# PSUM banks of three mixers in two pairs, a new plan for their steps, and one norm for both halves of the linear attention

## The chip, the cores and the metric

The kernel runs on one core of a Trainium2 chip. The metric is the device time of one launch in microseconds (us), 803.68 as the median of three runs before the change (801.09, 803.68 and 803.68). A core has the engines TensorE (PE, matmuls; PEld is its weight load), VectorE (DVE), ScalarE (ACT), GpSimd (POOL) and SyncE (SP, which here only starts transfers). Each engine works through its own list of instructions in order. Matmuls write PSUM, which here is eight banks of 128 partitions x 512 numbers; everything else lies in SBUF.

## The reference, cut to what matters

Two layers run over 256 tokens of width 1024. In each, one normed input is projected to 3 groups of columns; three mixers work on them, and their outputs, 512 wide each, are joined and projected back. A gated feed-forward and a gated side input follow.

```python
for i in range(2):
    a = rms_norm(h, attn_norm[i])
    (da_q, da_k, da_v, ssd_z, ssd_xbc, ssd_dt, gla_q, gla_k, gla_v, gla_g, gla_lr) = split(a @ w_in[i])
    y_da  = diff_attention(...)  # 4 heads: softmax(q1 k1) - lam * softmax(q2 k2), causal, times v, rms_norm
    y_ssd = ssd_mixer(...)       # state-space scan, 2 chunks of 128 tokens
    y_gla = gla_mixer(...)       # linear attention with decay, 4 heads of 128, 4 chunks of 64 tokens
    h = h + concat(y_da, y_ssd, y_gla) @ w_out[i]
    f = rms_norm(h, ffn_norm[i])
    h = h + (silu(f @ w_ffn_gate[i]) * (f @ w_ffn_up[i])) @ w_ffn_down[i]
    h = h + sigmoid(h @ ple_w_gate[i]) * (p[i] @ ple_w_proj[i])

# the end of gla_mixer; o is (tokens, 4 heads, 128)
o = rms_norm(o, g_norm) * silu(g_out)      # the mean square is over the 128 numbers of a head
```

## The kernel before

All weights come from memory as fp32 and are split on the core: ScalarE copies a tile to a rounded high part `wh` (L214), VectorE subtracts to get the low part `wl` (L215). Both have six buffers, so a split waits until the matmuls of an older tile have read theirs. A projection unit is a run of matmuls with high and low parts into one of four PSUM banks tagged `acc` (lines L242 to L265 and L884 to L886, by unit). The units follow each other without a pause when nothing holds them, and the mixers' work is laid between them.

The mixers are Python generators: `da` (the differential attention), `ssd` (the state-space scan) and `gla` (the linear attention, with a step of its own for the decays, L740 to L756). Each `yield` ends a step. The table `PLAN` names the units of the input projection in order and, for each, which mixer goes on one step after which of the unit's pieces (`-` is none); `PLAN_OUT` does so for the units of the output projection. So the tables set the order in which the work is issued; a scheduler then makes each engine's list from it, with small moves for what is marked `soon()`, and gives out buffers. An instruction that needs a buffer waits until the last reader of that buffer is done.

The mixers' matmuls write four PSUM banks tagged `mix` (`bank()`, names `pm`), used in turn by all three. The steps that matter here, with their names:

- `ssd` transposes its inputs (L599, one bank), which VectorE reads at L601 and L602. Later it multiplies (L639) and VectorE finishes at L644 and L645.
- the decays: a triangular matmul (L752) into one bank, which ScalarE reads twice, with a table load for the exponential before the first (`ex` L755, `ei` L756).
- `gla`: scores (L772) into two banks `pa`; chunk states (L790) into three banks `pst`, which VectorE reads one after the other (L804 for the first, L802 for the others, L807 scales); the output in two banks `po` (L817 within the chunk, L826 from the states); norm and gate; transposes (L845); then high and low part of the four `mix` tiles (L409 on ScalarE, L410 on VectorE), which the output projection reads at L256.
- `da`: score units u1 (rows 0 to 127, four heads), u2 and u3 (rows 128 to 255, two heads each). Each writes two banks `pb`, one per softmax, with 64-row matmuls L484 that go to the two banks in turn, and a mask (L491); VectorE takes the maxima (L499), ScalarE the exponentials `e` (L504), VectorE scales and subtracts (L507 to L512). The result is transposed (L469), copied to `at` (L471) and multiplied with `v` (L536, L540, L541) into the bank `y`; norm; transposes (L526); mix parts.

The norm of a bank is `head_norm`: a square on ScalarE (L395), a sum over each head (L397), then 1/sqrt on VectorE by twelve small operations on 128x4 numbers (L184 to L194), and one multiplication of 128x512 numbers (L402). `gla` calls it for each of its two banks and multiplies by the gate afterwards (L837, two halves each).

```python
for e in range(2):
    yn = head_norm(po[e])
    for b in range(2):
        y = yn.rearrange("p (j b d) -> p j b d", j=2, b=2)[:, :, b]
        g = sg[b].rearrange("p (j e d) -> p j e d", j=2, e=2)[:, :, e]
        dve.tensor_tensor(y, y, g, ALU.mult)
    ys.append(yn)
```

Of the kernel before, what the change touches and what calls it, by code (L numbers as in the profile page):

```python
# [10 lines left out]
F32 = mybir.dt.float32  # L11
# [9 lines left out]
P = 128  # L21
# [64 lines left out]
    ('gv0', ('ssd',)),  # L86
    ('gv1', ('gla', '-', '-', 'da', 'da')),
    ('sg0', ('gla', 'ssd', 'gla')),
    ('sg1', ('-', 'da', 'ssd')),
    ('v0', ('ssd', '-', 'da', '-', 'da')),  # L90
    ('v1', ('ssd', 'da', '-', 'gla')),
    ('ple', ('da', '-', '-', 'da', '-', 'gla')),
]
PLAN_OUT = [('-', '-', 'da'), ('-', '-', 'da'), ('-', '-', 'da'), (), (), ()]


def _two_pi_parts():
# [11 lines left out]
def trunk_kernel(ctx: ExitStack, tc: tile.TileContext, a: dict):  # L109
# [21 lines left out]
    def bank_acc():  # L131
        return ps.tile([P, 512], F32, tag="acc", bufs=NACC, name=nm("acc"))

    def bank():
        return ps.tile([P, 512], F32, tag="mix", bufs=8 - NACC, name=nm("pm"))

    def v3(ap, n):
        return ap.rearrange("p (a b) -> p a b", a=n)
# [278 lines left out]
    def da_gen(i, S):  # L417
# [55 lines left out]

        for qb, heads in units:
            nh, nk = len(heads), P * (qb + 1)
            pb = [bank(), bank()]
            for j, hd in enumerate(heads):
                q, k = qk[hd // 2], qk[2 + hd // 2]
                o = (hd % 2) * T

                for n, (a_, b_) in enumerate(((0, 0), (0, 1), (1, 0))):
                    for c in range(2):
                        r = slice(64 * c, 64 * c + 64)
                        pe.matmul(pb[c][:, j * nk:(j + 1) * nk], q[a_][r, o + qb * P:o + (qb + 1) * P],  # L484
                                  k[b_][r, o:o + nk], start=j == 0 and n == 0, stop=False,
                                  skip_group_check=True)
                if j < nh - 1:
                    yield 'part'
            for c in range(2):

                pe.matmul(v3(pb[c], nh)[:, :, nk - P:], idb, negb.unsqueeze(1).to_broadcast([P, nh, P]),  # L491
                          start=False, stop=True, skip_group_check=True)
            if len(es_of) == 2:
                yield 'part'
                attn_t(es_of[0])
            mx = small("mx", [P, 2, 4])
            es, sm = [], small("sm", [P, 2, 4])
            for c in range(2):
                dve.tensor_reduce(mx[:, c, :nh], v3(pb[c], nh), AX.X, ALU.max)  # L499
            dve.tensor_scalar(mx[:, :, :nh], mx[:, :, :nh], -0.125, None, op0=ALU.mult)  # L500
            for c in range(2):
                e = slot("e")
                for j in range(nh):
                    act.activation(e[:, j * nk:(j + 1) * nk], pb[c][:, j * nk:(j + 1) * nk], AF.Exp,  # L504
                                   bias=mx[:, c, j:j + 1], scale=0.125, accum_out=sm[:, c, j:j + 1])
                es.append(e)
            dve.reciprocal(sm[:, :, :nh], sm[:, :, :nh])  # L507
            dve.tensor_scalar(sm[:, 1, :nh], sm[:, 1, :nh], lam[:, i:i + 1], None, op0=ALU.mult)
            for j in range(nh):
                s = slice(j * nk, (j + 1) * nk)  # L510
                dve.tensor_scalar(es[1][:, s], es[1][:, s], sm[:, 1, j:j + 1], None, op0=ALU.mult)
                dve.scalar_tensor_tensor(es[0][:, s], es[0][:, s], sm[:, 0, j:j + 1], es[1][:, s],  # L512
                                         ALU.mult, ALU.add)
            es_of.append(es[0])
            yield
# [12 lines left out]
                parts(m, qb * P, pt[:, hd * P:(hd + 1) * P], gcol)  # L528

        for qb in range(2):  # L530
            y = bank()
            for hd in range(4):
                o = y[:, hd * P:(hd + 1) * P]
                vs = slice(hd * P, (hd + 1) * P)
                if qb == 0:
                    pe.matmul(o, at[0][:, hd * P:(hd + 1) * P], v[0][:, vs], start=True, stop=True)  # L536
                else:
                    t = at[1 + hd // 2]
                    j = 2 * (hd % 2)
                    pe.matmul(o, t[:, j * P:(j + 1) * P], v[0][:, vs], start=True, stop=False)  # L540
                    pe.matmul(o, t[:, (j + 1) * P:(j + 2) * P], v[1][:, vs], start=False, stop=True)  # L541
                if hd == 1:
                    yield 'part'
            ys.append(head_norm(y))
            yield
# [214 lines left out]
    def gla_gen(i, S):  # L760
# [1 line left out]
        dve.tensor_tensor(q, q, ex, ALU.mult)  # L762
        dve.tensor_tensor(k, k, ei, ALU.mult)
        yield
        pa = [bank(), bank()]
        for j in range(2):
            for b in range(2):
                o = (2 * j + b) * P
# [14 lines left out]
        yield  # L783

        v = S["gv"]
        pst = [bank() for _ in range(3)]
        for j in range(2):
            for c in (0, 1, 2):
                b, r = c // 2, slice(64 * (c % 2), 64 * (c % 2) + 64)
# [17 lines left out]
                dve.tensor_scalar(sv[:, j], sv[:, j], ex[:, col:col + 1], None, op0=ALU.mult)  # L807
            prev.append(st)
        yield
        po = [bank(), bank()]  # L810

        for j in range(2):
            for b in range(2):
# [6 lines left out]
        for j in range(2):  # L820
# [7 lines left out]
                              skip_group_check=True)  # L828
            if j == 0:
                yield 'part'  # L830
        ys, sg = [], S["sg"]
        for e in range(2):
            yn = head_norm(po[e])
            for b in range(2):
                y = yn.rearrange("p (j b d) -> p j b d", j=2, b=2)[:, :, b]
                g = sg[b].rearrange("p (j e d) -> p j e d", j=2, e=2)[:, :, e]
                dve.tensor_tensor(y, y, g, ALU.mult)  # L837
            ys.append(yn)
        yield
        gcol = par[i][:, O_GLAN:O_GLAN + 1]  # L840
# [405 lines left out]
```

## Time and profile before

| | |
|---|---|
| median of three runs | 803.68 us |
| the profiled execution | 800.33 us |
| its span, first to last instruction | 798.1 us |
| mean granted clock of TensorE | 0.999 of full speed |
| PE busy | 778.2 us, 98% |
| DVE busy | 640.9 us, 80% |
| ACT busy | 477.4 us, 60% |
| chain of work that ended last | PE 80%, DVE 14%, DMA 2%, ACT 2% |

The profiled execution lies 2.2 us above its span and is faster than any of the three timed runs. Busy time is the union of an engine's instructions; what is not busy is a wait or a gap. The chain is followed back from the last instruction, at each step to what released it or to the instruction before it on its engine. A row of a time line gives start, duration, engine, line of the kernel, operation, what it writes and reads, and in brackets how long the engine stood idle before it and for what. Matmuls overlap, so the distance of two starts, not the duration, is what one matmul takes of TensorE's time. The first layer's input projection with the mixers lies at 60 to 165 us, the second layer's at 455 to 560 us, in the same order some 392.5 us later.

### The profile page before, as it was taken

The numbers are of one execution on the slowest core, as the hardware profiler recorded it, in microseconds if no ns is written. First come the engines' busy times: TensorE is split into PE (matmuls) and PEld (weight loads), VectorE is DVE, ScalarE is ACT, GpSimd is POOL, SyncE is SP. The second block draws the span as 40 slices with busy tenths as digits, with TensorE's granted clock in tenths as the row PEclk, the third lists the DMA queues.
The fourth block names the chain that finished last, engine by engine and source line by source line (L and its number), as shares of the span: only waits on it lengthen the run. The fifth ranks groups of instructions, "written<-read, shape, count | busy, mean of one in ns | idle before, by whom it ended". The sixth has DMA issues, their size and how long they took to land.

```text
span 798.1 us, 12793 instructions
## 1 busy us (share of the span) xinstructions
PE 778.2 (98%) x4810; PEld 682.7 (86%) x4810; DVE 640.9 (80%) x1341; ACT 477.4 (60%) x838; POOL 23.1 (3%) x36
## 2 busy tenths in 40 slices
PE   9999999899999999999999999997999999999997
PEld 6998877789888888888889988786998888888887
DVE  5998998888787777667799779988897777767674
ACT  7778537656665555555667585285466555554553
POOL 2000000002000000000020000000020000000000
PEclk9999999999999999999999999999999999999999
DMA  8763524244655543557555523433455555445641
GB/s 292 284 218 111 172 84 153 82 159 159 211 197 178 206 154 135 184 185 248 208 168 202 172 96 127 159 106 106 168 179 185 207 173 196 159 148 183 198 158 54
DMA packets 24302, 134.92 MB, mean 169 GB/s; under 512 B 2992, under 2 KB 5296, under 8 KB 11696
## 3 DMA queue, kind: packets, MB, share of 16 engines
q1 hardware_dynamic: 23904, 133.57, 48.8%
q8 instruction: 38, 0.62, 0.3%
q0 software_dynamic: 192, 0.52, 0.2%
q14 instruction: 24, 0.20, 0.1%
q10 hardware_dynamic: 144, 0.01, 0.0%
HBM read 133.05 MB, written 1.05 MB: 168 GB/s over the span
## 4 chain that ended last, share of the span: by engine, by line
PE 80%; DVE 14%; DMA 2%; ACT 2%; issue 1%; SPq 0%; DVEq 0%; ACTq 0%
PE acc L256 37%; PE acc L258 18%; DVE wl L215 4%; PE acc L265 4%; PE acc L264 4%; PE acc L263 4%; PE acc L884 2%; PE acc L886 2%; PE acc L885 2%; ACT e L504 1%; DMA h<-in_x 1%; PE acc L243 1%; PE acc L242 1%; PE acc L244 1%; DMA st<-in_w_z 1%
## 5 line engine op out<-in xcount | busy, mean ns | idle before, releaser
L214 ACT ACTIVATE wh<-st 128x1024 fp32r<-128x1024 f32 (+5 forms) x274 | 266.9, 979 | 231.0 <-PE acc L256 101.3
L215 DVE TENSOR_TENSOR wl<-st,wh 128x1024 fp32r<-128x1024 f32 (+5 forms) x274 | 308.5, 1128 | 100.3 <-ACT wh L214 99.8
L256 PE MATMUL acc<-x,wh 128*128 128x512 f32 x800 | 252.2, 396 | 0.1
L258 PEld LDWEIGHTS acc<-x,wl 128*128 128x128 f32 x800 | 150.3, 188 | 35.2
L258 PE MATMUL acc<-x,wl 128*128 128x256 f32 x800 | 157.2, 278 | 0.0
L256 PEld LDWEIGHTS acc<-x,wh 128*128 128x128 f32 x800 | 122.2, 189 | 1.4 <-DVE x L296 0.7
L256 PE MATMUL acc<-act,wh 128*128 128x512 f32 x352 | 111.9, 395 | 0.0
L258 PEld LDWEIGHTS acc<-act,wl 128*128 128x128 f32 x352 | 66.2, 188 | 14.3
L258 PE MATMUL acc<-act,wl 128*128 128x256 f32 x352 | 72.0, 279 | 0.0
L884 PE MATMUL acc<-wh,x 128*128 128x512 f32 x160 | 66.8, 420 | 0.5 <-DVE gate L301 0.4
L265 PE MATMUL acc<-x,wl 128*128 128x256 f32 x224 | 63.4, 283 | 0.9 <-DVE wl L215 0.9
L263 PE MATMUL acc<-x,wh 128*128 128x256 f32 x224 | 63.8, 285 | 0.0
L886 PE MATMUL acc<-wh,x 128*128 128x512 f32 x160 | 63.6, 397 | 0.0
L885 PE MATMUL acc<-wl,x 128*128 128x512 f32 x160 | 63.3, 396 | 0.2 <-DVE wl L215 0.2
L264 PE MATMUL acc<-x,wh 128*128 128x256 f32 x224 | 63.4, 283 | 0.0
L256 PEld LDWEIGHTS acc<-act,wh 128*128 128x128 f32 x352 | 54.9, 189 | 1.3
L265 PEld LDWEIGHTS acc<-x,wl 128*128 128x128 f32 x224 | 42.9, 192 | 1.1 <-DVE wl L215 1.1
L264 PEld LDWEIGHTS acc<-x,wh 128*128 128x128 f32 x224 | 42.9, 192 | 0.3
L263 PEld LDWEIGHTS acc<-x,wh 128*128 128x128 f32 x224 | 42.9, 191 | 0.3
L256 PE MATMUL acc<-mix,wh 128*128 128x512 f32 x128 | 40.8, 401 | 2.3 <-DVE mix L410 2.3
L301 DVE TENSOR_TENSOR gu<-acc,gu 128x256 f32<-128x256 f32 x88 | 36.8, 418 | 2.9 <-ACT gu L300 2.9
L884 PEld LDWEIGHTS acc<-wh,x 128*128 128x128 f32 x160 | 30.3, 190 | 6.9 <-ACT wh L214 0.7
(276 smaller groups left out, 1166.7 us busy)
## 6 DMA issues: line engine op xcount, KB each, us to landing
st<-in_w_f SPq DMA_DIRECT2D x44, 1024.0 KB, 4.9
st<-in_w_d SPq DMA_DIRECT2D x32, 704.0 KB, 4.1
st<-in_w_x SPq DMA_DIRECT2D x18, 1024.0 KB, 4.8
st<-in_w_o SPq DMA_DIRECT2D x12, 1024.0 KB, 5.0
st<-in_w_t SPq DMA_DIRECT2D x11, 1024.0 KB, 4.9
st<-in_w_g SPq DMA_DIRECT2D x8, 1024.0 KB, 4.9
st<-in_w_z SPq DMA_DIRECT2D x3, 1088.0 KB, 5.0
st<-in_w_x SPq DMA_DIRECT2D x8, 256.0 KB, 5.0
```

Source lines behind the costliest of these rows:

```text
L214: i_hi = act.activation(wh[:, s], st[:, o], AF.Copy)
L215: i_lo = dve.tensor_tensor(wl[:, s], st[:, o], wh[:, s].bitcast(F32), ALU.subtract)
L242: pe.matmul(out, sh, mh, start=i == 0, stop=False)
L256: pe.matmul(out, wh[:, lo:lo + P], x[k], start=k == 0, stop=False)
L258: last = pe.matmul(out[:, :T], wl[:, lo:lo + P], x[k][:, :T], start=False, stop=k == n - 1)
L263: pe.matmul(out, sh, hi, start=k == 0, stop=False)
L264: pe.matmul(out, sh, x[k][:, T:], start=False, stop=False)
L265: last = pe.matmul(out[:, :T], sl, hi, start=False, stop=k == n - 1)
L301: dve.tensor_tensor(out, pb[:, :T], out, ALU.add)
L884: pe.matmul(pb[b], xh, wh, start=kk_ == 0, stop=False)
L885: pe.matmul(pb[b], xh, wl, start=False, stop=False)
L886: last = pe.matmul(pb[b], xl, wh, start=False, stop=kk_ == KD - 1)
```

## The change

`bank()` keeps two of the four banks, and a new `held_bank()` has the other two (names `ph`). Held banks are used for `da`'s scores `pb` and its output `y`, and for `gla`'s scores `pa`, the first two chunk states and its output `po`. All else (transposes, the decays, `ssd`, the third chunk state) takes the two others. The tables lay steps of `ssd` and `da` at other pieces, and two more steps of `da` go into the units of the output projection. `gla` gets its own norm: two squares, two sums into one 128x8 tile, one 1/sqrt for both banks, and then eight operations of 128x128 numbers that scale and gate at once, reading PSUM. Per layer VectorE has ten instructions fewer. The new lines move later ones: up to the norm a line of the new kernel is 4 more than the same line before (L488 is L484), behind it 14 more (L859 is L845); the new norm is L840 to L849.

```diff
@@ the tables (two of the five changed lines) @@
-    ('v1', ('ssd', 'da', '-', 'gla')),
+    ('v1', ('-', '-', 'da', '-', 'gla')),
-PLAN_OUT = [('-', '-', 'da'), ('-', '-', 'da'), ('-', '-', 'da'), (), (), ()]
+PLAN_OUT = [('-', 'da', '-', '-', 'da'), ('-', '-', '-', '-', 'da'), ('-', '-', 'da'), (), (), ()]
@@ the banks @@
     def bank():
-        return ps.tile([P, 512], F32, tag="mix", bufs=8 - NACC, name=nm("pm"))
+        return ps.tile([P, 512], F32, tag="mix", bufs=2, name=nm("pm"))
+
+    def held_bank():
+        return ps.tile([P, 512], F32, tag="held", bufs=6 - NACC, name=nm("ph"))
...
-            pb = [bank(), bank()]
+            pb = [held_bank(), held_bank()]
...
-            y = bank()
+            y = held_bank()
...
-        pa = [bank(), bank()]
+        pa = [held_bank(), held_bank()]
...
-        pst = [bank() for _ in range(3)]
+        pst = [held_bank(), held_bank(), bank()]
...
-        po = [bank(), bank()]
+        po = [held_bank(), held_bank()]
@@ the norm of the linear attention @@
         ys, sg = [], S["sg"]
+        ss, f = small("gss", [P, 8]), small("gf", [P, 8])
         for e in range(2):
-            yn = head_norm(po[e])
-            for b in range(2):
-                y = yn.rearrange("p (j b d) -> p j b d", j=2, b=2)[:, :, b]
-                g = sg[b].rearrange("p (j e d) -> p j e d", j=2, e=2)[:, :, e]
-                dve.tensor_tensor(y, y, g, ALU.mult)
+            sq = slot("fsq")
+            act.activation(sq, po[e], AF.Square)
+            dve.tensor_reduce(ss[:, 4 * e:4 * e + 4], v3(sq, 4), AX.X, ALU.add)
+        with soon():
+            rsqrt(f, ss, [P, 8], 1.0 / P, EPS)
+        for e in range(2):
+            yn = slot("fyn")
+            for j in range(2):
+                for b in range(2):
+                    n, o = 2 * j + b, (2 * j + e) * P
+                    dve.scalar_tensor_tensor(yn[:, n * P:(n + 1) * P], po[e][:, n * P:(n + 1) * P],
+                                             f[:, 4 * e + n:4 * e + n + 1], sg[b][:, o:o + P],
+                                             ALU.mult, ALU.mult)
             ys.append(yn)
```

Three places show how the engines' lists move. The first is ScalarE in the first layer, where the decays' exponentials stand near two splits of one weight tile; before:

```order
L214 ACTIVATE wh_182_1142<-st_181_1141 128x1024
L755 ACT_TABLE_LOAD
L755 ACTIVATE ex_144_968<-pm_143_963 128x512
L756 ACTIVATE ei_145_969<-pm_143_963 128x512
L214 ACTIVATE wh_184_1147<-st_181_1141 128x1024
L387 ACTIVATE dsq_151_997<-acc_122_877 128x256
```

and now (L218 is L214, L759 and L760 are L755 and L756):

```order
L218 ACTIVATE wh_182_1142<-st_181_1141 128x1024
L218 ACTIVATE wh_184_1147<-st_181_1141 128x1024
L759 ACT_TABLE_LOAD
L759 ACTIVATE ex_144_968<-pm_143_963 128x512
L760 ACTIVATE ei_145_969<-pm_143_963 128x512
L391 ACTIVATE dsq_151_997<-acc_122_877 128x256
```

The split `wh_184` now stands ahead of the table load and of both reads of the bank `pm_143`. On TensorE the second pair of `ssd`'s transposes (L599) takes that bank next, since only two are left to take turns; it stood behind L752, L681 and one more matmul of a unit, and now stands behind the end of that unit and the first 18 matmuls of the next.

The second place is TensorE at the scores u1 of the first layer, where `pm_252`, `pm_253` (now `ph_`) are the banks of the two softmaxes and `qh`, `ql` high and low parts of q and k; before:

```order
L790 MATMUL pm_243_1377<-gv_223_1305,kx_234_1343 128x256
L484 MATMUL pm_252_1421<-qh_217_1285,qh_211_1261 128x128
L484 MATMUL pm_252_1421<-ql_218_1286,qh_211_1261 128x128
L484 MATMUL pm_253_1422<-qh_217_1285,qh_211_1261 128x128
L484 MATMUL pm_253_1422<-ql_218_1286,qh_211_1261 128x128
L484 MATMUL pm_252_1421<-qh_217_1285,ql_212_1262 128x128
L484 MATMUL pm_253_1422<-qh_217_1285,ql_212_1262 128x128
```

and now (L488 is L484, L898 to L900 are unit matmuls):

```order
L900 MATMUL acc_230_1319<-wh_225_1309,x_16_165 128x512
L488 MATMUL ph_252_1421<-qh_220_1297,qh_214_1273 128x128
L488 MATMUL ph_252_1421<-ql_221_1298,qh_214_1273 128x128
L488 MATMUL ph_252_1421<-qh_220_1297,ql_215_1274 128x128
L898 MATMUL acc_229_1318<-wh_227_1314,x_19_174 128x512
L899 MATMUL acc_229_1318<-wh_228_1315,x_19_174 128x512
L900 MATMUL acc_229_1318<-wh_227_1314,x_19_174 128x512
L488 MATMUL ph_252_1421<-qh_220_1297,qh_214_1273 128x128
L488 MATMUL ph_252_1421<-ql_221_1298,qh_214_1273 128x128
L488 MATMUL ph_253_1422<-qh_217_1285,qh_211_1261 128x128
L488 MATMUL ph_253_1422<-ql_218_1286,qh_211_1261 128x128
```

The matmuls of the second softmax have moved behind nearly all of the first; its bank is now that of the second chunk state (L802 reads it last), where the list before took banks by age.

The third place is VectorE at the norm of the linear attention; before (`pm_300` and `pm_301` are the banks `po`, `sg` the gate):

```order
L194 SCALAR_TENSOR_TENSOR ff_304_1731<-rs_t_307_1734,ff_304_1731 128x4
L402 TENSOR_TENSOR fyn_305_1732<-pm_300_1696,ff_304_1731 128x512
L397 TENSOR_REDUCE fss_309_1752<-fsq_308_1750 128x4
L837 TENSOR_TENSOR fyn_305_1732<-fyn_305_1732,sg_264_1524 128x2x128
L184 TENSOR_SCALAR rs_v_312_1756<-fss_309_1752 128x4
L837 TENSOR_TENSOR fyn_305_1732<-fyn_305_1732,sg_265_1525 128x2x128
L188 TENSOR_SCALAR ff_310_1754<-rs_v_312_1756 128x4
```

and now (L198 ends the one 1/sqrt, L849 scales and gates):

```order
L196 TENSOR_TENSOR rs_t_307_1739<-gf_303_1731 128x8
L197 SCALAR_TENSOR_TENSOR rs_t_307_1739<-rs_t_307_1739,rs_v_306_1738 128x8
L198 SCALAR_TENSOR_TENSOR gf_303_1731<-rs_t_307_1739,gf_303_1731 128x8
L849 SCALAR_TENSOR_TENSOR fyn_308_1752<-ph_300_1699,gf_303_1731,sg_269_1541 128x128
L849 SCALAR_TENSOR_TENSOR fyn_308_1752<-ph_300_1699,gf_303_1731,sg_270_1542 128x128
```

The second chain of twelve and the four products L837 are gone from the list; L849 (two more for this bank, four for `ph_301`) takes the place of both L402, and the mix parts of the linear attention (L410 before) follow directly.

## Rows read from the trace of the kernel before

**Rows 1.** The page, busy time of each engine, us (share of the span) and instructions.

```profile
PE 778.2 (98%) x4810; PEld 682.7 (86%) x4810; DVE 640.9 (80%) x1341; ACT 477.4 (60%) x838; POOL 23.1 (3%) x36
```

**Rows 2.** Stretches: us, then busy time of each engine, granted clock, DMA.

```profile
...
60.00:165.00 105.00, 98.97 (x622) 82.98 (x622) 94.42 (x254) 64.52 (x124) 0.10 (x1) 1.00 0.37 124
165.00:395.00 230.00, 229.94 (x1355) 201.87 (x1354) 174.77 (x306) 132.12 (x228) 5.18 (x3) 1.00 0.55 185
...
455.00:560.00 105.00, 99.24 (x618) 83.16 (x617) 94.24 (x247) 64.39 (x123) 0.00 (x0) 1.00 0.34 117
...
```

**Rows 3.** TensorE waits: instruction <- releaser: us in total, times, longest.

```profile
...
PE pm L845 <- DVE fyn L837: 4.1, 2, 2.0
PE pm L536 <- ACT v L912: 2.5, 2, 1.2
PE acc L256 <- DVE mix L410: 2.3, 2, 1.2
...
```

**Rows 4.** Time line of ScalarE, first layer: start, us, engine, line, operation.

```profile
...
74.83 1.28 ACT L755 ACT_TABLE_LOAD   x1
...
76.62 0.59 ACT L756 ACTIVATE ei<-pm 128x512 f32<-128x512 f32 x1
77.22 1.06 ACT L214 ACTIVATE wh<-st 128x1024 fp32r<-128x1024 f32 x1
```

**Rows 5.** Time line of TensorE in the same place.

```profile
...
75.89 0.60 PE L599 MATMUL pm<-cst,conv 128*128 128x128 f32 x4
...
76.79 0.39 PE L886 MATMUL acc<-wh,x 128*128 128x512 f32 x1
...
79.06 0.28 PE L265 MATMUL acc<-x,wl 128*128 128x256 f32 x1
...
```

**Rows 6.** Time line of VectorE, the state copies of the linear attention.

```profile
...
112.90 0.85 DVE L804 COPY gst<-pm 64x256 f32<-64x256 f32 x2
...
116.57 0.86 DVE L802 TENSOR_TENSOR gst<-pm,gst 64x256 f32<-64x256 f32 x2
...
```

**Rows 7.** Time line of TensorE, scores on two banks in turn.

```profile
...
113.90 0.29 PE L484 MATMUL pm<-qh,qh 64*128 64x128 f32 x1 [0.50 <-DVE gst L804]
113.91 0.32 PE L484 MATMUL pm<-qh,ql 64*128 64x128 f32 x1
...
```

**Rows 8.** Time line of TensorE, scores of one bank alone.

```profile
...
129.53 0.38 PE L484 MATMUL pm<-qh,qh 64*128 64x256 f32 x1
129.75 0.28 PE L484 MATMUL pm<-ql,qh 64*128 64x256 f32 x1
...
```

**Rows 9.** Time line of ScalarE, exponentials and the square of the linear attention.

```profile
...
139.33 0.48 ACT L504 ACTIVATE e<-pm,mx 128x256 f32<-128x256 f32 x1
...
141.86 0.49 ACT L504 ACTIVATE e<-pm,mx 128x256 f32<-128x256 f32 x1
...
145.14 0.60 ACT L395 ACTIVATE fsq<-pm 128x512 f32<-128x512 f32 x1 [0.76 <-PE pm L826]
...
```

**Rows 10.** Time line of VectorE, the norm of the linear attention.

```profile
...
150.79 0.16 DVE L184 TENSOR_SCALAR rs_v<-fss 128x4 f32<-128x4 f32 x1
...
153.16 0.16 DVE L194 SCALAR_TENSOR_TENSOR ff<-rs_t,ff 128x4 f32<-128x4 f32 x1
153.43 0.69 DVE L402 TENSOR_TENSOR fyn<-pm,ff 128x512 f32<-128x512 f32 x1
154.16 0.76 DVE L837 TENSOR_TENSOR fyn<-fyn,sg 128x256 f32<-128x256 f32 x2
...
```

**Rows 11.** Time line of TensorE, the last two waits of the stretch.

```profile
...
154.73 0.79 PE L845 MATMUL pm<-cst,fyn 128*128 128x128 f32 x4 [2.03 <-DVE fyn L837]
...
161.26 0.96 PE L256 MATMUL acc<-mix,wh 128*128 128x512 f32 x3 [1.15 <-DVE mix L410]
```

**Rows 12.** Groups of 60 to 165 us: line, operation, shapes, count | busy, mean ns.

```profile
...
L410 DVE SCALAR_TENSOR_TENSOR mix<-pm,par,mix 128x128 fp32r<-128x128 f32 x8 | 2.8, 346 | 0.0
...
L194 DVE SCALAR_TENSOR_TENSOR ff<-rs_t,ff 128x4 f32<-128x4 f32 x9 | 1.5, 162 | 0.3
...
```

More of the change, by code (lines that the diff above doesn't have):

```diff
@@ L88 @@
     ('sg0', ('gla', 'ssd', 'gla')),
-    ('sg1', ('-', 'da', 'ssd')),
-    ('v0', ('ssd', '-', 'da', '-', 'da')),
-    ('v1', ('ssd', 'da', '-', 'gla')),
-    ('ple', ('da', '-', '-', 'da', '-', 'gla')),
+    ('sg1', ('-', 'da', 'ssd', 'ssd')),
+    ('v0', ('-', 'da', '-', 'ssd', 'da')),
+    ('v1', ('-', '-', 'da', '-', 'gla')),
+    ('ple', ('-', 'da', '-', '-', '-', 'gla')),
 ]
-PLAN_OUT = [('-', '-', 'da'), ('-', '-', 'da'), ('-', '-', 'da'), (), (), ()]
+PLAN_OUT = [('-', 'da', '-', '-', 'da'), ('-', '-', '-', '-', 'da'), ('-', '-', 'da'), (), (), ()]
 def _two_pi_parts():
```

## The prediction

> **What bounds the kernel now.** I read the busy times first [rows 1]: TensorE is busy 778.2 of 798.1 us, so whatever the change does to other engines shows only where TensorE waits. The table of stretches says where that can be [rows 2]: between the mixers (165 to 395 us) TensorE is busy 229.94 of 230 us; beside the mixers it loses 6.03 us in the first layer and 5.76 us in the second, 11.8 together. The change touches nothing else, so 11.8 us is all that it can win. VectorE is busy 94 of 105 us there [rows 2]: it is nearly full, and a delay on it is not soon made up. The list of waits says what for [rows 3]: per layer 2.05 us for the gated norm of the linear attention (L845 after L837), 1.25 us for `da`'s `v` (L536) and 1.15 us for the last mix parts of the linear attention (L256), 4.45 us in all, and all three lie behind the linear attention's output, within 146 to 162 us.
>
> **The norm.** Before: the first square starts at 145.14 [rows 9], the last gate product ends at 154.92 [rows 10], 9.8 us for two banks one after the other. The root of the second bank takes from 150.79 to 153.32, with a gate product between its twelve operations; L402 and two gate products follow, 1.5 us [rows 10]. After, with both banks ready at once: two squares (0.6 each), the second sum ends 1.8 us after the start, then twelve operations on 128x8 numbers. None of these is in the trace. A 128x4 one takes 162 ns [rows 12] and the next starts after 0.20 (150.79 to 153.16, less the product). Lower bound 12 x 0.20 = 2.4, upper bound twice that for twice the numbers, 4.8; I take 2.4, since the instruction's fixed part dominates at this size. The scale-and-gate operation is nearest to the 128x128 mix part L410, which also reads PSUM and a second tensor, at 346 ns [rows 12]; eight cost 2.8 us without overlap and 8 x 0.26 = 2.1 with the overlap that neighbours have. Four of them release the first transposes: 1.05 (bound above 1.4). Sum 0.1 + 1.8 + 2.4 + 1.05 = 5.35 us from output to first transposes, against 9.6 to the second ones before [rows 9, 11]. VectorE has ten instructions fewer, some 3 us less work per layer.
>
> **The held pair.** All score units of `da`, then `po`, then `y` take turns in one pair. u3's scores therefore start when u2's exponentials end, 139.8 in the trace before [rows 9], where they had other banks. Scores and mask take 2.0 us, the maxima on VectorE with the mix parts that stand between them 2.3 (an estimate: two sums like those of the norm and three operations like L410 [rows 12]), four exponentials of 0.45 end at about 146.0, against 142.35 before [rows 9]. The eight L817 and twelve L826 matmuls need 2.2 us from there: the linear attention's output is ready at 148.25, not 145.1 (bounds: 145.1, if the pair is free as early as before, and 149.5, if the exponentials wait for one more table load of 1.28 us [rows 4]). TensorE is not idle for all 3.1 us, since unit matmuls moved ahead: counted matmul by matmul, what the new list has issued by then had been issued by 146.4 before, so it is 1.85 behind. Of that, 0.3 comes from u1, which waits for the second chunk state's bank (L802 at 116.57 releases it, not L804 at 112.90 [rows 6]) and loses the pairing: matmuls for two banks start 0.01 us apart [rows 7], for one bank 0.12 to 0.22 [rows 8]. The rest of u1's 1.5 us is covered by the wait of u2 for u1's exponentials, which exists already.
>
> Then the norm: ready at 148.25 + 5.35 = 153.6. TensorE arrives after four transposes and twelve unit matmuls at 150.3 and waits 3.3 us. Behind it the second transposes, the mix parts and L256 find everything done: the matmuls of `ssd`'s part and the first `y` take until 160.0, the mix parts of the linear attention are there by 159.2. So 1.85 + 3.3 replace the 4.45 us of [rows 3] with the small losses at the same places (0.15 each): 5.15 - 4.9 = about +0.3 to +0.6 us; I take +0.5.
>
> **The split ahead of the table load.** TensorE's second pair of L599 needs the bank that L756 gives back. Before, it started at 75.89 without a wait [rows 5]. Now the split `wh_184` stands ahead of the load. Its buffer is that of `wh_120`, last read at 76.79 [rows 5], 76.4 without the moved transposes; read ends 76.85, split 1.0, load 1.28, `ex` 0.5, `ei` 0.59 [rows 4]: 80.2. TensorE arrives at 79.06 + 0.12 - 0.35 = 78.83 [rows 5] and waits 1.4 us. Bounds: none, if the buffer is free at 74.83 and all comes 1 us later than before; 1.8, if the split starts at 77.22 as before [rows 4]. Queued behind it are unit matmuls, and VectorE's L601 and L602, which read the bank. TensorE's own loss is soaked up by the later waits on VectorE, but VectorE ends its run 0.7 to 0.9 us later: +0.8 per layer (0 to 1.4).
>
> On this load the row shows 1.28 us, and `ei`, the second exponential behind it, starts 0.51 us after its end [rows 4], so nothing else stands around it. The Trainium skill, ScalarE: Activation LUTs, section What ACT_TABLE_LOAD costs, adds a drain of about 1.38 us to a load of 1.28 us. By that rule L599 would wait 2.8 us and the forecast would rise by up to 2.8 us for two layers. This case's trace agrees on the load (1.28 us) and shows no drain, so I give the rule no chance of its own.
>
> **The out units.** Two steps of `da` move into them. Transposes L526 need norms that VectorE has finished less than 1 us earlier by my count; I cost them at nothing, hidden by the output projection's own matmuls, and at 0.5 to 1 us per layer if VectorE comes that much later.
>
> **Sum.** 0.5 + 0.8 = 1.3 us per layer, 2.7 for two: 800.3 becomes 803.0. The median shown is 803.68, 3.4 above the profiled execution, and the four executions known lie between 800.3 and 803.7; the forecast is placed with the middle of both readings (803.0 and 803.7 + 2.7 = 806.4): 804.7 us.
>
> **Rivals.** *Faster.* The norm's gain is kept: ScalarE finishes u3's exponentials early enough that the output is ready near 146, and the three waits of 4.45 us [rows 3] go but for 1 us. For it: the chain shrinks by over 4 us, and it is the place where TensorE waits longest. Against: 3.1 us of it are given back by the held pair. It gives -3.5 per layer for the norm, +0.8 for the split, -5.4 in all: 798.3 on the median; without the split's wait 796.7.
>
> *Slower.* The held pair as a chain: u1, u2, u3, `po` and `y` each wait for the last reader of the one before, on ScalarE and VectorE. If u2's exponentials come behind the two table loads that stand ahead of them in the new list, by 1.28 us each [rows 4] more than I count, then everything from u3 to `y` moves 2.6 us per layer, and TensorE has nothing left to put there: 2 x 2.6 + 2.7 = 7.9, 808.2 on the profiled execution and 811.6 on the median. It decides from where u3's exponentials end behind 147.5 us. Against: in the trace before, ScalarE is busy 64.5 of 105 us in the stretch [rows 2] and has time to catch up. Beside this stands the rule of the Trainium skill, Perfetto Trace Analysis, Matmul Optimizations, to use all eight PSUM banks so that more can run at once: two groups of two give a tile fewer banks to choose from. No run so far shows which of the two is worth more here.
>
> *Nothing.* The waits change places and their sum stays: 800.3 to 803.7.
>
> **How the numbers follow.** What a measurement of this kernel can tell from no change is about 0.5%, 4.0 us: faster is below 799.7, slower above 807.7. My sum has a chance of 0.40 (0.35 of it within 0.5%, 0.02 and 0.03 to the sides), nothing 0.19, faster 0.20, slower 0.21: same 0.54, faster 0.22, slower 0.24. The upper bounds of the output (149.5, so 2 x 1.25) and of the split (2 x 0.4, and 2 x 0.6 that it then costs VectorE) put the forecast at 809.2, the lower ones (the pair free early, no wait at L599) lead into the faster case. The range is 797.5 to 809.5: it leaves out the lower third of the faster case and more than half of the slower one, 0.07 and 0.12.
>
> **What would show it.** Right: L599 waits about 1.4 us for the exponential near 79 us; in u1 the second softmax's scores wait for the second chunk state (L802, then L806) and its matmuls start singly; the square of the norm starts at 148, three us later than before; one wait of some 3 us at the first L845 (then L859) in place of three. Wrong: the square starts by 146 (then the faster case), or a new wait above 2 us stands at u2 or u3 (then the slower), or the stretch from 165 us on, full before [rows 2], shows waits for `da`'s norms.

## The result, and the profile after

The changed kernel takes 807.7 us in the median of seven runs (807.23 to 812.1), the one before 802.6 in seven runs of its own (800.36 to 803.68): 5.1 us more, a ratio of 1.0081 with a 95% interval of 1.0062 to 1.0100. Forecast were 804.7 us and no change; the time lies inside the range, and 5.1 us are a little more than the 4.0 us that the prediction counts as no change.

The profiled execution took 812.1 us at a mean granted clock of 0.989; five of the seven lie between 807.2 and 807.9 at 0.995 or 0.996. So some 4.4 us of what the profile shows more is not in the median, and what they are will come out below. The page's busy times (engine, us, share of the span, instructions):

```profile
...
PE 790.2 (98%) x4810; PEld 691.1 (85%) x4810; DVE 638.4 (79%) x1321; ACT 478.0 (59%) x838; POOL 23.1 (3%) x36
...
```

TensorE is as full as before, 98%, but of a longer span; VectorE has 2.5 us less work [rows 1]. By stretches (us, then busy time and instructions of PE, PEld, DVE, ACT, POOL, granted clock, DMA share and GB/s):

```profile
...
60.00:165.00 105.00, 99.78 (x566) 82.29 (x566) 86.02 (x224) 61.98 (x121) 0.10 (x1) 0.93 0.32 113
165.00:395.00 230.00, 229.97 (x1363) 202.30 (x1362) 175.12 (x314) 128.97 (x221) 5.18 (x3) 1.00 0.54 183
...
455.00:560.00 105.00, 99.28 (x607) 82.78 (x606) 85.92 (x213) 63.05 (x121) 0.00 (x0) 0.99 0.35 123
...
```

The stretch between the mixers is full again, 229.97 of 230 us [rows 2], so the two added steps of the output units cost TensorE nothing. The new thing is the clock column: 0.93 and 0.99 in the two mixer stretches, where the kernel before had 1.00. TensorE's waits (instruction, releaser: us in total, times, longest):

```profile
...
PE pm L859 <- DVE fyn L849: 2.9, 2, 1.4
PE pm L603 <- ACT ei L760: 2.8, 2, 1.4
PE acc L246 <- ACT v L926: 2.0, 2, 1.0
...
PE ph L821 <- ACT e L508: 1.5, 2, 0.7
PE ph L488 <- DVE gst L806: 1.3, 2, 0.7
...
```

The three largest waits of before, 8.9 us [rows 3], are replaced by the first four, 9.2 us. Two of them the prediction named by place (L603, L859); L821, where the output waits for u3's exponentials, it had only as time lost; and L246 waiting for `v` it did not have. The fifth, u1's, stood before too, 1.2 us in all behind L804. TensorE does not idle more: if its idle time in the second layer's stretch is added up between the same two unit matmuls (455.13 to 567.28 us before, 462.93 to 579.14 after), it is the same to 0.04 us; in the first layer (71.87 to 174.86 us before, 71.76 to 182.68 after) it is 0.8 us less. The second layer's stretch is nevertheless 4.1 us longer. So TensorE does not wait more there, its matmuls take longer.

**The split ahead of the table load.** ScalarE (first layer; start, us, engine, line, operation) and the transposes on TensorE:

```profile
...
76.50 1.07 ACT L218 ACTIVATE wh<-st 128x1024 fp32r<-128x1024 f32 x1 [1.93 <-PE acc L900]
77.58 1.28 ACT L759 ACT_TABLE_LOAD   x1
...
79.37 0.59 ACT L760 ACTIVATE ei<-pm 128x512 f32<-128x512 f32 x1
...
```

```profile
...
80.02 0.66 PE L603 MATMUL pm<-cst,conv 128*128 128x128 f32 x4 [1.41 <-ACT ei L760]
...
```

As forecast, the split waits for its buffer, then come 1.28 us of table load, and `ei` ends just when L603 starts: at 80.02 after an idle time of 1.41 us (forecast 80.2 and 1.4; without a wait before [rows 5]). The next activation follows the load at 78.88, so here too nothing stands behind it.

**The linear attention's norm in the second layer.** ScalarE's last exponential of u3, the two squares and the copy of `v`:

```profile
...
547.83 0.48 ACT L508 ACTIVATE e<-ph,mx 128x256 f32<-128x256 f32 x1
...
551.03 1.09 ACT L840 ACTIVATE fsq<-ph 128x512 f32<-128x512 f32 x2 [2.14 <-PE ph L830]
552.01 1.27 ACT L926 ACTIVATE v<-acc,rcol 128x512 f32<-128x512 f32 x2
...
```

The first square of this layer in the kernel before:

```profile
...
537.53 0.60 ACT L395 ACTIVATE fsq<-pm 128x512 f32<-128x512 f32 x1 [0.76 <-PE pm L826]
...
```

VectorE's root (first and last of twelve) and the eight scale-and-gate operations:

```profile
...
552.98 0.17 DVE L188 TENSOR_SCALAR rs_v<-gss 128x8 f32<-128x8 f32 x1
...
555.20 0.17 DVE L198 SCALAR_TENSOR_TENSOR gf<-rs_t,gf 128x8 f32<-128x8 f32 x1
555.48 2.16 DVE L849 SCALAR_TENSOR_TENSOR fyn<-ph,gf,sg 128x128 f32<-128x128 f32 x8
...
```

TensorE's two waits:

```profile
...
552.75 0.38 PE L246 MATMUL acc<-ph,wh 128*128 128x256 f32 x1 [1.00 <-ACT v L926]
...
555.88 1.10 PE L859 MATMUL pm<-cst,fyn 128*128 128x128 f32 x4 [1.44 <-DVE fyn L849]
...
```

The sizes of the new operations were right: twelve operations of 0.17 us at a pitch of 0.20, eight of L849 in 2.16 us, 0.27 each. From the first square to L859 it takes 4.85 us (forecast 5.35), against 9.6 before. But the square comes at 551.03; before it came at 537.53, and 7.8 us of the difference lie ahead of this layer's mixers, so it is 5.7 us late, not 3.1. u3's exponentials end at 548.31, which is 148.1 in the first layer's time of before (7.8 and the layers' distance of 392.4 us off), not 146.0. And ScalarE, in order, copies `v` behind both squares: L246 waits 1.00 us for the accumulator bank that this frees.

**Matmuls that take longer.** The small matmuls of the second layer's mixers (line, shapes, count | busy, mean ns of one | idle before), of the kernel before and of the changed one:

```profile
...
L790 PE MATMUL pm<-gv,kx 64*128 64x256 f32 x12 | 2.0, 401 | 0.0
...
L484 PE MATMUL pm<-qh,qh 64*128 64x128 f32 x8 | 1.7, 330 | 0.7 <-DVE gst L804 0.7
...
L772 PE MATMUL pm<-gq,gkk 64*128 64x128 f32 x16 | 1.5, 287 | 0.0
...
L826 PE MATMUL pm<-gst,gq 64*64 64x128 f32 x24 | 1.1, 282 | 0.0
...
```

```profile
...
L488 PE MATMUL ph<-qh,qh 64*128 64x128 f32 x8 | 2.3, 291 | 0.7 <-DVE gst L806 0.7
...
L776 PE MATMUL ph<-gq,gkk 64*128 64x128 f32 x16 | 1.9, 310 | 0.0
...
L794 PE MATMUL ph<-gv,kx 64*128 64x256 f32 x8 | 1.8, 415 | 0.0
...
L830 PE MATMUL ph<-gst,gq 64*64 64x128 f32 x24 | 1.5, 284 | 0.0
...
L794 PE MATMUL pm<-gv,kx 64*128 64x256 f32 x4 | 1.1, 402 | 0.0
...
```

The mean of one changes little (L484 is 39 ns shorter, the others at most 23 ns longer), but the time in which they are under way is longer. Part of that only says that other matmuls stand between them. What a group takes of TensorE's time is the distance from each of its starts to the next start, less idle time: added up, this layer's 48 matmuls of L484 (now L488) went from 6.01 to 6.42 us, the chunk states L790 (now L794) from 1.64 to 2.12, L826 from 1.02 to 1.37 and L772 from 1.46 to 1.70, 1.5 us together; the last three are the same in the first layer. They overlap less. At u1 the trace shows it (first layer):

```profile
...
119.84 0.29 PE L488 MATMUL ph<-qh,qh 64*128 64x128 f32 x1 [0.66 <-DVE gst L806]
119.97 0.28 PE L488 MATMUL ph<-ql,qh 64*128 64x128 f32 x1
120.09 0.27 PE L488 MATMUL ph<-qh,ql 64*128 64x128 f32 x1
...
```

Consecutive matmuls now go to one bank and start 0.12 us apart; before, two started 0.01 us apart on two banks [rows 7]. The two banks belong to the two softmaxes, which also use different 64 rows of q and k; no run separates which of the two lets matmuls start together. Adding up these distances for all matmuls between the same two unit matmuls as above gives 4.1 us more in the second layer, of which the low clock below takes at most 1.7, and 8.7 more in the first, of which it takes at most 6.8: at least 2.4 and 1.9 us are lost in matmuls that follow each other less closely.

**The clock.** In windows of 1 us (same columns as the stretches):

```profile
...
119.00:120.00 1.00, 0.34 (x4) 0.23 (x3) 0.96 (x3) 0.00 (x0) 0.00 (x0) 1.00 0.45 74
120.00:121.00 1.00, 1.00 (x9) 1.00 (x8) 1.00 (x2) 0.00 (x0) 0.00 (x0) 0.63 0.54 156
121.00:122.00 1.00, 1.00 (x7) 1.00 (x6) 1.00 (x3) 0.00 (x0) 0.00 (x0) 0.50 0.95 401
...
129.00:130.00 1.00, 1.00 (x4) 0.81 (x4) 0.84 (x2) 0.44 (x3) 0.00 (x0) 0.50 0.00 0
130.00:131.00 1.00, 1.00 (x7) 0.80 (x6) 0.93 (x4) 0.37 (x2) 0.00 (x0) 0.75 0.00 0
131.00:132.00 1.00, 1.00 (x6) 0.77 (x5) 1.00 (x5) 1.00 (x6) 0.00 (x0) 1.00 0.03 8
...
```

At 120.26 us, 0.4 us after the wait at u1 ended, the granted clock falls from 1.00 to 0.50, that is from 2.4 to 1.2 GHz, and stays there until 130.50, for 10.24 us in which TensorE is busy all the time. Two more such stretches of 3.41 us lie behind L859, at 161 us and, in the second layer, at 557 us. The profile of the kernel before has one only in its last 2.2 us, where TensorE is done. Half of a low stretch, where TensorE has work, is lost: 8.5 us at most in this execution. Its runs at 0.995 have less.

### The profile page after: what moved, and what is told of

The parts are those of the page before. It is cut to its first block, busy times and chain, and to the rows that moved or that the text cites. A ratio compares the mean times of both kernels' runs of the same rounds, so it can differ in the third digit from the quotient of the medians.

```text
span 810.0 us, 12774 instructions
## 1 busy us (share of the span) xinstructions
PE 790.2 (98%) x4810; PEld 691.1 (85%) x4810; DVE 638.4 (79%) x1321; ACT 478.0 (59%) x838; POOL 23.1 (3%) x36
## 4 chain that ended last, share of the span: by engine, by line
PE 90%; DVE 5%; DMA 2%; ACT 2%; issue 1%; SPq 0%; ACTq 0%; DVEq 0%
PE acc L260 37%; PE acc L262 18%; PE acc L898 4%; PE acc L900 4%; PE acc L899 4%; PE acc L269 4%; PE acc L267 4%; PE acc L268 4%; DVE wl L219 2%; DMA st<-in_w_x 1%; PE acc L247 1%; PE acc L246 1%; PE acc L248 1%; PE ph L488 1%; PE pm L643 1%
## 5 line engine op out<-in xcount | busy, mean ns | idle before, releaser
L218 ACT ACTIVATE wh<-st 128x1024 fp32r<-128x1024 f32 (+5 forms) x274 | 267.4, 980 | 223.6 <-PE acc L260 102.7
L898 PE MATMUL acc<-wh,x 128*128 128x512 f32 x160 | 66.0, 414 | 1.0 <-ACT wh L218 0.6
L900 PE MATMUL acc<-wh,x 128*128 128x512 f32 x160 | 64.6, 404 | 0.0
L898 PEld LDWEIGHTS acc<-wh,x 128*128 128x128 f32 x160 | 30.5, 191 | 7.5 <-ACT wh L218 1.3
```

The source lines that it names most:

```text
L218: i_hi = act.activation(wh[:, s], st[:, o], AF.Copy)
L898: pe.matmul(pb[b], xh, wh, start=kk_ == 0, stop=False)
L900: last = pe.matmul(pb[b], xl, wh, start=False, stop=kk_ == KD - 1)
```

## The experiments

Every run has its own runs of the kernel before beside it: 801.36 us in the first four, 801.57 in the next four, 802.66 in the last three.

**The three edits apart.** `norm_only` is the kernel before with the new norm; `plan_norm` takes the changed kernel and gives all four banks to one pool; `banks_only` is the kernel before with the pairs; `banks_plan` is the changed kernel with the old norm.

```diff
@@ plan_norm @@
     def bank():
-        return ps.tile([P, 512], F32, tag="mix", bufs=2, name=nm("pm"))
-
-    def held_bank():
-        return ps.tile([P, 512], F32, tag="held", bufs=6 - NACC, name=nm("ph"))
+        return ps.tile([P, 512], F32, tag="mix", bufs=8 - NACC, name=nm("pm"))
...
-            pb = [held_bank(), held_bank()]
+            pb = [bank(), bank()]
...
```

The other calls of `held_bank()` become `bank()` in the same way.

> The kernel before with the new norm of the linear attention alone (old banks, old plan). Theory A (the 5 us come from banks and plan: TensorE's small matmuls lose their neighbours and its clock falls for some us, while the norm helps): 1 to 4 us faster than before, the waits at L845 and at the last mix parts (2.05 and 1.15 us a layer) shrink to under 1 us, granted clock 0.998 or more. Theory B (the one root costs, since no product can start before both sums): 1 to 3 us slower, with a wait at L845 of 2 us or more.

Measured: 797.72 us, ratio 0.9946 (0.9929 to 0.9963), faster than both kernels. Its waits:

```profile
...
PE pm L536 <- ACT v L921: 1.8, 2, 0.9
PE acc L256 <- DVE mix L410: 1.7, 2, 0.9
...
PE pm L854 <- DVE fyn L844: 0.4, 2, 0.2
...
```

L845 (here L854) waits 0.4 us in all instead of 4.1, the other two 3.5 instead of 4.8 [rows 3]. Theory A holds in time and waits, not in the clock (0.994 to 0.999 instead of 0.998 or more): with neither pairs nor new plan the profile has a low stretch of 6.83 us behind u1, at 506.3 us. Theory B falls: one root for both banks gains, though nothing can start before both sums.

> The changed kernel with the four mixers' banks in one pool again (new plan, new norm). Theory A, if the pairs break up the scores: L484 and L790 take some 0.9 us less of TensorE per layer than in the changed kernel, 2 to 4 us faster than it, so 1 to 3 us slower than before. If the plan alone breaks the groups: as the changed kernel, 807 to 808. Theory C (the held pair delays u3 and the output): the square of the norm starts near 146 instead of 152 us and 3 us per layer are won, 800 to 802.

Measured: 801.84 us, 0.9998 (0.9985 to 1.0012): as before. Against the changed kernel (807.7) one pool gains 5.9 us; against the norm alone the plan loses 4.1. Its waits at the norm are nearly those of the changed kernel:

```profile
...
PE pm L854 <- DVE fyn L844: 2.9, 2, 1.5
PE acc L242 <- ACT v L921: 2.3, 2, 1.2
PE pm L817 <- ACT e L504: 2.0, 2, 1.0
...
```

So these do not come from the pair: with one pool, too, `v` stands behind the squares and little else beside the norm. Nor is it the pair alone that makes u3 late: L817 waits for u3's exponentials here, too. How much the plan does is read best from `plan_only` (below; one pool, new plan), whose first layer has no low clock ahead of the square. The last exponential of u3 and the squares there:

```profile
...
145.81 0.49 ACT L504 ACTIVATE e<-pm,mx 128x256 f32<-128x256 f32 x1
...
148.63 1.09 ACT L395 ACTIVATE fsq<-pm 128x512 f32<-128x512 f32 x2 [1.76 <-PE pm L826]
...
```

This layer starts 0.5 us later than before, and the square comes 3.5 us after the 145.14 of before [rows 9]: of the 5.7 us in the changed kernel the plan makes some 3.0, and 2.7 are left for the pairs, the wait at L603 among them. (In the second layer of `plan_norm` the square is 3.9 us late, but a low stretch of 6.83 us stands ahead of it.)

Theory C gets the total right by luck: its square is still late, at 148.44 us and not near 146. Theory A has the reason: with one pool L772, L790 and L826 take 1.48, 1.64 and 1.02 us per layer again, as before. All distances together, with half of each low stretch taken off, are 2.5 us less than in the changed kernel in the first layer and 3.5 in the second, by this estimate the whole of the 5.9 us; A's 2 to 4 us were too few.

> The kernel before with the banks in two pairs alone (old plan, old norm). Theory A: 2 to 5 us slower than before, by more time of TensorE in L484 and L790, not by waits. Theory C: 4 to 8 us slower, by waits at L484 of u2 and u3 and at L817 of over 1 us each, since the old plan asks for the pair earlier.

Measured: 813.79 us, 1.0153 (1.0135 to 1.0171), worse than either theory said. The wait behind it:

```profile
...
PE ph L540 <- DVE fyn L406: 8.2, 2, 4.1
...
```

The old plan asks for `y` (L540, L536 before) right behind the linear attention's output, and both use the pair: `y` waits 4.1 us per layer until the norm has read it. Theory A's loss is there as well: L772 and L790 take 1.70 and 2.12 us per layer, as in the changed kernel, while L826 keeps its 1.02.

> The changed kernel with the old norm (two roots, gate afterwards). Theory A: 3 to 6 us slower than the changed kernel, 811 to 814, since L845 comes 4 us later per layer and the waits of the kernel before return. Theory B: as fast as the changed kernel or faster, 805 to 808.

Measured: 819.05 us, 1.0219 (1.0200 to 1.0238). With the old norm the changed kernel is 11.4 us slower, more than theory A said and more than the norm gains alone (3.6). The transposes (L850 here) wait 3.6 us per layer for the norm, against 1.4 in the changed kernel:

```profile
...
PE pm L850 <- DVE rs_v L188: 4.3, 2, 2.2
...
PE pm L850 <- DVE fyn L842: 2.8, 2, 1.4
...
```

That is 4.2 us of the 11.4; its clock is lower, too (0.981 to 0.985), and how the rest divides is not shown.

**The two cells left**, `banks_norm` (the changed kernel with the old tables) and `plan_only` (the kernel before with the new tables):

> The changed kernel with the old plan (two pairs of banks, new norm). If the new plan suits the pairs: 808 to 813, slower than the changed kernel by up to 5 us. If the plan costs here what it costs with one pool (4.1 us, 801.84 against 797.72): 803 to 805.

Measured: 815.40 us, 1.0167 (1.0138 to 1.0195). Neither number was right; it is beyond the upper one. The wait for `y` is 5.2 us per layer here:

```profile
...
PE ph L540 <- DVE fyn L849: 10.3, 2, 5.2
...
```

> The kernel before with the new plan alone (one pool, old norm). If the plan's cost is its own (4.1 us with the new norm): 804.5 to 807. If the plan costs only because the norm's gain has no room left beside it: 801 to 803.

Measured: 811.1 us, 1.0104 (1.0084 to 1.0125), slower than both expectations. Its largest waits:

```profile
...
PE pm L845 <- DVE rs_v L184: 4.3, 2, 2.2
PE pm L845 <- DVE fyn L837: 3.5, 2, 2.1
...
```

The whole of it, medians in us:

| | old plan | new plan |
|---|---|---|
| one pool, old norm | 801.4 to 802.7 | 811.1 |
| one pool, new norm | 797.7 | 801.8 |
| pairs, old norm | 813.8 | 819.05 |
| pairs, new norm | 815.4 | 807.7 |

From one cell to the next, the norm (-3.6), the plan (+4.1) and the pairs (+5.9) lead from 801.4 to 807.7. The pairs cost with either plan and either norm. The plan costs with one pool and helps (7.7 us) only with pairs and new norm, where it takes `y` away from the pair's queue; with the old norm that wait goes as well, but those at L850 come. The new norm gains 3.6 to 11.4 us, but not with the pairs under the old plan, where `y` waits for both sums: there the two intervals overlap.

**The wait at L603 alone.** `after_tm_held` is the changed kernel with these transposes in held banks, which are free then; the exponentials stand ahead of the split again.

```diff
         def token_major(b):
-            pb = bank()
+            pb = held_bank()
```

> The changed kernel with the banks of ssd's input transposes (L603, L599 before) taken from the held pair, so that they no longer wait for the exponentials behind the weight split. If the wait of 1.4 us per layer reaches the end: 2 to 3 us faster than the changed kernel, 804.7 to 806. If later waits on VectorE soak it up: 806.5 to 808, with longer waits at u1 and L821.

Measured: 808.28 us, no better than the changed kernel. But the wait at L603 is gone and the others are as they were:

```profile
...
PE pm L859 <- DVE fyn L849: 2.9, 2, 1.4
...
PE ph L488 <- DVE gst L806: 1.3, 2, 0.7
...
```

The runs differ by their clock: at 0.996 it takes 804.60 and 804.63 us, where the changed kernel takes 807.70; at 0.989 it takes 808.28 and 808.62 against 811.89 and 812.10; at 0.983 and 0.984 it takes 813.12 and 811.38, and the changed kernel had no run that low. At equal clock the two waits are worth 3.1 to 3.8 us, somewhat more than the first theory said, and the lower clock took them back: 0.990 in the mean of its seven runs, against 0.993. Why it is lower is not shown.

**u1's banks.** `after_pst` goes on from there: only the first chunk state is held, so u1 finds both banks early.

```diff
-        pst = [held_bank(), held_bank(), bank()]
+        pst = [held_bank(), bank(), bank()]
```

> The changed kernel with L603's banks held (as in the run before) and only the first chunk state held, so that u1 finds both its banks early and its matmuls alternate again. If the held pair's remaining cost is u1's wait and the lost alternation: L484's wait of 0.7 us goes, L484 and L790 take some 0.9 us less per layer, and at equal clock it is 1.5 to 3 us faster than the run before (at a clock of 0.996 801.6 to 803.1 instead of 804.6). If it is the queue u2, u3, output on one pair: as the run before, 804.6 at that clock.

Measured: 803.68 us, 1.0016 (0.9999 to 1.0032). The wait at u1 is gone, one at u2 of 1.5 us per layer has come:

```profile
...
PE ph L488 <- ACT e L508: 3.0, 2, 1.5
PE pm L859 <- DVE fyn L849: 2.9, 2, 1.4
...
```

At equal clock nothing is gained (804.72 at 0.995 against 804.6 at 0.996): the second theory holds there, since u2 waits for u1's exponentials anyway. But the twelve runs have a mean clock of 0.997 instead of 0.990, and the 4.6 us between the medians go with it. In the profiled execution one low stretch of 3.4 us is left, where the run before had two of 10.24 us behind u1 and two of 3.4. In all thirteen profiles every low stretch of 10.24 us, seven in number, begins at u1 in a kernel whose u1 matmuls go to one bank at a time; all others, but those at the end of the kernel, last 3.41 or 6.83 us. That the order decides the length is likely, but this run changed the wait at u1 with it, so it is not shown.

The first layer of this profile has no low stretch, and there the distances of all matmuls still add up to 2.3 us more than before (99.20 against 96.95), with 1.4 us less idle time. So the lost overlap is not the clock's. L484 is nearly back (5.97 us against 5.75 before), L790 is not (2.32).

**Dummy matmuls in the waits.** `after_fill`, `norm_fill` and `norm_fill_less` add matmuls whose result is overwritten, ahead of the first real one into the bank.

```diff
+    def fill(bank_, n):
+        for _ in range(n):
+            pe.matmul(v3(bank_, 4), idb, negb.unsqueeze(1).to_broadcast([P, 4, P]), start=True, stop=True, ...)
@@ norm_fill @@
             pb = [bank(), bank()]
+            fill(pb[0], 3 if len(es_of) < 2 else 0)
...
             y = bank()
+            fill(y, 4)
```

> The changed kernel with dummy matmuls (bf16, 512 columns, overwritten afterwards) ahead of the first norm's transposes L859 (6) and ahead of u1 and u2 (3 each), in the time in which TensorE waits. Theory A1 (the low clock follows TensorE's idle time): the low stretches at 161 and 557 us vanish, the mean clock rises to 0.998, 2 to 3.5 us faster than the changed kernel, 804 to 806. Rival (the low clock comes with the small matmuls, not with the idle time): clock as in the changed kernel, 807.5 to 809.5.

Measured: 808.89 us, mean clock 0.993. In the profiled execution the low stretches behind L859 are gone as theory A1 said, the one of 10.24 us behind u1 is still there and one of 3.4 us has come in the second layer. The dummies ahead of u1 stand in front of its first bank, and its wait for the second (0.55 us behind the chunk state) is still there. So the low stretches went where the idle time was filled and stayed where it was not, which speaks for theory A1; the mean clock and the time are what the rival said, and there is no gain.

> The norm alone on the kernel before, with dummy matmuls ahead of u1 and u2 (3 each), L536 and L541 (4 each) and the first L845 (1), in the time in which TensorE waits. Theory A1: no low stretch but at the end, clock 0.998, 1 to 3 us faster than the norm alone, 794.5 to 796.5. Rival: as the norm alone or up to 2 us slower, 797.5 to 800.

Measured: 799.76 us, 0.9978 (0.9968 to 0.9989), 2 us slower than the norm alone. The clock rose as expected (0.998 in the mean of twelve runs, against 0.996), but the dummies brought a wait that the norm alone does not have:

```profile
...
PE pm L490 <- DVE mix L415: 2.6, 2, 1.3
...
```

> The norm alone with fewer dummy matmuls: ahead of u1 (2) and of L536 and L541 (3 each), none ahead of u2 and L845. If the dummies of u2 and L845 were what cost time in the run with more of them and the rest keeps the clock up: 795.5 to 797.2. If any dummy costs what it takes: 798 to 800.

Measured: 797.64 us, 0.9934 (0.9915 to 0.9952), the same as the norm alone and between the two expectations. Its profiled execution (span, mean clock):

```profile
core 0: 795.4 us, clock 1.000
...
```

All six runs have 0.999 or 1.000, all within 797.24 to 797.88. The norm alone has 795.81 and 796.00 at 0.999 and 797.59 to 798.84 at 0.994 to 0.996. So work in the idle time does hold the clock up, and here costs what it wins, some 1.7 us; the runs only become alike.

## Why the prediction was right or wrong

**The bound.** Right: only the mixers' stretches changed, and the stretch from 165 us on stayed full.

**The split ahead of the load.** Right to 0.2 us in place and size. Its price at the end was mis-sized: forecast 0.8 us per layer, since later waits on VectorE should soak up the rest; 1.5 to 1.9 us measured at equal clock. Little was soaked up.

**The norm.** Right in its operations (4.85 us for 5.35), and it gains: with one pool and the old plan it is worth 3.6 us. That the rival "faster" names 796.7 without the split's wait and the norm alone took 797.7 is luck: the rival takes off 7.0 us. VectorE has 1.25 us less work per layer, not some 3.

**The held pair.** Here the prediction failed, in the step that counted TensorE "1.85 behind" at the output, of which "0.3 comes from u1", while u2's wait covers the rest. That count took the new list at the pace of the old and put u3's delay down to the pair alone. The output was 5.7 us late instead of 3.1 in the second layer, some 3.0 of it by the plan, which one pool with the new plan shows. The one wait of 3.3 us at L859 stood there as three, at L821 (0.73), L246 (1.00, for the copy of `v` behind the squares, which the sum did not have) and L859 (1.44). These together, 3.2, are less than the 4.45 us they replace; with L603's 1.4 the idle time is the same. What came on top is some 2 us per layer (1.9 and 2.4 at least) of matmuls that overlap less, and one pool gives it back. Lost pairing was in the sum, for u1 alone, and as good as covered.

**The clock.** It was in no step and no rival. The profile before shows 1.00 in both mixer stretches [rows 2], and I took it as given, though waits of 1 to 2 us stand there. The runs of the kernel before, which came with the experiments, have clocks of 0.990 to 0.999, and none is above the 0.999 of its profiled execution. But the clock is not what separates the two medians: the mean over the runs is 0.993 for the changed kernel and 0.993 to 0.994 for the one before, and at 0.995 the kernel before takes 800.68 to 802.72 us (19 runs, 801.4 in the median), the changed one 807.23 to 807.91 (four runs), some 6 us more.

**The sum.** Forecast 1.3 us per layer (2.7 for two, by rounding). Between the same unit matmuls the first layer's stretch takes 102.99 us before and 110.92 after, the second 112.15 and 116.22; with half of the low stretches (6.8 and 1.7 us) taken off, 1.1 and 2.4 us are left, 3.5 against 2.7 forecast. Waits behind a low stretch take up some of it, so 3.5 is the least. What is missing to the 5.1 us of the medians can't be told from one profile of each. The time lies inside the range, 1.8 us from its upper end, but not the change: by the prediction's own 4.0 us, 5.1 are slower and not the same. That the range held for a sum without the plan's delay and most of the lost overlap is in part luck. Of its signs of being right the wait at L599 and u1's single matmuls came as written, the square at 148 and the one wait of 3 us did not; none of its signs of being wrong came.

**The rival "slower"** was nearer than I gave it (0.21). Its point was passed: u3's exponentials end at 148.1 in the first layer's time, behind 147.5. Its place was half right: the pair as a queue is dear only where the plan does not keep `y` away from it (4.1 and 5.2 us per layer in `banks_only` and `banks_norm`); in the changed kernel the plan moves u3 about as much as the pairs do. And its price was too high: 807.7 lies between the forecast and its 811.6.

**Left open:** what in the order makes L772, L790 and L826 overlap less. L772 and L790 lose with the pairs under either plan, L826 only with pairs and new plan together (1.02 us in `banks_only` and `plan_norm`, 1.37 in the changed kernel); the alternation of banks was restored for u1 only.

## What to carry to other kernels

Before a pool is split, ask which two long-held tiles then queue for one pair, and try each part of a change alone: here the norm gains 0.5%, and pools and plan take it and more away. Where small matmuls run in pairs, an order that separates them costs TensorE time that no list of waits shows; add up the distances between starts. Where TensorE waits for a microsecond here and there, look at the granted clock of several runs, since one profile may show the lucky one, and compare two kernels at equal clock.

## What the runs showed of the hardware

The granted clock fell to half for 3.41, 6.83 or 10.24 us at a time, in the changed kernel's profile 0.4 to 1.8 us behind the end of an idle time of TensorE, and with the same kernel in some executions more than in others: the kernel before ran at mean clocks from 0.990 (803.1 to 804.8 us) to 0.999 (800.77). There the low stretch began while TensorE was busy again; in `banks_only` one began within the wait for `y` (at 154.43 us, the wait from 151.30 to 155.38). In all thirteen profiles each one among the mixers began within an idle time of 0.5 us or more or at most 2.9 us behind its end. An idle time alone does not bring it: the profile before has waits of up to 2.0 us [rows 3] and no low stretch among the mixers. Dummy matmuls in the idle time held the clock at 0.999 or more in six of six runs, against two of six without them.
